# Strassen products for 44 of the 72 blocks of an input projection, with one pool of tiles that all phases share

## The chip, the cores and the metric

The kernel runs on one core of one Trainium2 chip. The metric is the device time of one execution in microseconds (us). The core has TensorE (PE: matrix multiplies; PEld are its weight loads), VectorE (DVE), ScalarE (ACT), GpSimd (POOL) and SyncE (SP, which here issues the loads). They run beside each other, each through its own instructions in order, and wait for each other on semaphores.

## The reference

One decoder block on 512 tokens with 16 meta tokens ahead of them (528 columns), 1024 channels. Cut to what matters:

```python
u = rmsnorm(h, attn_norm_w)
proj = u @ w_in                                   # 1024 -> 9 x 1024
q, f_raw, i_in, g_out, b_gate, c_gate, x_conv, gate_a, gate_b = split(proj)
q = silu(q);  f = lb + (1 - lb) * sigmoid(f_raw);  k = 1 - f;  v = i_in
o = rmsnorm(hgrn2_chunked(q, k, v, log(f)), hgrn_norm_w)   # 8 heads, gated linear recurrence
y_a = o * silu(g_out)
y_b = b_gate * causal_dwconv(c_gate * x_conv, conv_w)      # width 3
h = h + (sigmoid(gate_a) * y_a + sigmoid(gate_b) * y_b) @ w_out
a, val = split(rmsnorm(h, ffn_norm_w) @ w_up)              # 1024 -> 2 x 2816
h = h + (silu(causal_dwconv(a, ffn_conv_w, ffn_conv_b)) * val) @ w_down
return rmsnorm(h, final_norm_w)[meta tokens dropped]
```

## The kernel before

Channels lie on the 128 partitions, tokens along the columns. All is float32. For a matrix multiply each operand is split into a high part, rounded to TensorE's fp32r, and a low part, the rest: `h = copy(x)` on ACT, `lo = x - h` on DVE. A product then takes three matmuls (high by high, high by low, low by high).

A **unit** is 128 output channels of one of the nine parts of w_in: 1024 x 128 weights, fetched with one DMA into `wr`, split into `wh` and `wl`. `w_in` has 72 units. `mtile` (L133) multiplies a unit with the 8 tiles `uh`, `ul` of the input (128 channels each, scaled by the norm's weight but not yet by its reciprocal root `rstd`) in two column spans of 256 to 264: 8 x 3 x 2 = 48 matmuls. The result, in one of the two 1024-wide accumulators `psm` of the pool `pmain`, is multiplied by `rstd` on DVE as it is taken out (`evac`, L155).

The program has these stages.

- Start: loads, the first three units (f, q, i of head 0), and `rstd`.
- Scan: for head j from 0 to 7, `fqi(j + 1)` runs the units f, q, i of the next head and `mix(j)` the units b, c, x, g, ga, gb of this one. The recurrence `recur(j)`, a generator with eight pieces of small matmuls, DVE products and masked copies, is woven in: `tick` takes its next piece after every few matmul groups.
- Output projection (L589): 8 units of w_out on the merged heads `mh`, `ml`, then the second norm.
- Feed-forward: 6 pairs of units of w_up by `mtile`, then 16 pairs as **Strassen pairs** (`pair_weights` L666, `product` L733, `Pair` L747): two units, each split in two along the 1024 inputs, are computed over two halves of the tokens with seven half-size products of 12 matmuls instead of eight. That needs sums of weight blocks (S1 to S4) and combinations of the input halves (`ch`, `cl`, from `combos`, L627), each split into high and low. The products go to three accumulators r1, r2, r3; r1 is added to again after a copy of it was kept (c1, c2, c3 by `keep`, L742). Between products, `more` puts blocks of the down projection.

A scheduler, not the text of the program, sets the final order on each engine: it places ready instructions by priority, so loads and splits of weights, and pieces of the recurrence, move ahead of where they are written.

Of the kernel before, what the change touches and what calls it, by code (L numbers as in the profile page):

```python
# [7 lines left out]
F32 = mybir.dt.float32  # L8
# [28 lines left out]
def unit_order():  # L37
    out = [(n, 0) for n in ("f", "q", "i")]
    for j in range(KT):
        if j + 1 < KT:  # L40
            out += [(n, j + 1) for n in ("f", "q", "i")]
        out += [(n, j) for n in ("b", "c", "x", "g", "ga", "gb")]
    return out
# [12 lines left out]
def block_kernel(ctx: ExitStack, tc: tile.TileContext, xT, par, wts, pairs, ident, masks, finw, out):  # L56
# [68 lines left out]
    mains = [pmain]  # L125
# [77 lines left out]
    xt = [xpool.tile([P, L], F32, name=f"xt{k}", tag=f"xt{k}") for k in range(KT)]  # L203
# [62 lines left out]
    mg_pool = ctx.enter_context(tc.tile_pool(name="mg", bufs=1, side="right"))  # L266
    mh = [mg_pool.tile([P, 516], F32R, name=f"mh{k}", tag=f"mh{k}")[:, :LT] for k in range(KT)]
    ml = [mg_pool.tile([P, 516], F32R, name=f"ml{k}", tag=f"ml{k}")[:, :LT] for k in range(KT)]
    ph = ExitStack()
    p1 = ph.enter_context(tc.tile_pool(name="ph1", bufs=1))  # L270
    z0 = [p1.tile([P, L], F32, name=f"z0{i}") for i in range(2)]
    uh = [p1.tile([P, L], F32R, name=f"uh{k}", tag=f"uh{k}") for k in range(KT)]
    ul = [p1.tile([P, L], F32R, name=f"ul{k}", tag=f"ul{k}") for k in range(KT)]
    rstd = p1.tile([P, L], F32, name="rstd")
    Ks = [p1.tile([P, L + 1], F32, name=f"K{i}") for i in range(2)]
    Vs = [p1.tile([P, L + 1], F32, name=f"V{i}") for i in range(2)]
    Fs = [p1.tile([P, L + 1], F32, name=f"F{i}") for i in range(2)]
    As = [p1.tile([P, NCH, P], F32, name=f"A{i}") for i in range(2)]
    Qs = [p1.tile([P, LT], F32, name=f"Q{i}") for i in range(2)]
    cx = p1.tile([P, LC], F32, name="cx")  # L280
    for i in range(2):
        nc.gpsimd.memset(Ks[i][:, L:], 0.0)
        nc.gpsimd.memset(Vs[i][:, L:], 0.0)
        nc.gpsimd.memset(Fs[i][:, L:], 1.0)
        nc.gpsimd.memset(As[i], 0.0)

    with tc.tile_pool(name="rp0", bufs=1) as rp:
        acc = rp.tile([P, L], F32, name="acc")
        firsts = [(split_unit(raw, 4), new_ps()) for raw, _ in heads]
        sides = ((FULL, L, z0[0]), (PART, LT, z0[1][:, :LT]))  # L290
        for k in range(KT):
            if k % 2 == 0:
                firsts[0][0][2][k // 2]()
            split_scaled(uh[k], ul[k], xt[k], pr("attn", k))
            if k % 2 == 0:
                firsts[1][0][2][k // 2]()
            for ((h, lo, _), ps), (spans, _, _) in zip(firsts, sides):
                mm3(ps, h[:, k, :], lo[:, k, :], uh[k], ul[k], spans, k == 0, k == KT - 1)
# [5 lines left out]
        for (_, ps), (spans, _, z) in zip(firsts, sides):  # L304
            act.copy(z, res(ps, spans))
        banks = [pqk.tile([P, NCH * P], F32, name="psq", tag="psq") for _ in range(2)]
        spread_rstd(rstd, acc, lambda i: banks[i], rp, L)
        act.copy(Vs[0][:, :L], res(mtile(uh, ul, FULL, (h3rd, l3rd)), FULL))
    p2 = ph.enter_context(tc.tile_pool(name="ph2", bufs=2))

    def sig(src, n):
        s = p2.tile([P, n], F32, name="sg", tag="sg")
        act.activation(s, src, AF.Sigmoid)
        return s

    def fqi(j):
        b = j % 2
        if j:
            ps = mtile(uh, ul, FULL)
            z = p2.tile([P, L], F32, name="z", tag="z")  # L320
            evac(ps, FULL, z, rstd)
        else:
            z = z0[0]
            dve.tensor_tensor(z, z, rstd, op=ALU.mult)
        s = sig(z, L)
        dve.tensor_scalar(Fs[b][:, :L], s, lbc[:, j:j + 1], lb[:, j:j + 1], op0=ALU.mult, op1=ALU.add)
        act.activation(Ks[b][:, :L], Fs[b][:, :L], AF.Identity, bias=one1, scale=-1.0)
        if j:
            ps = mtile(uh, ul, PART)
            z = p2.tile([P, L], F32, name="z", tag="z")[:, :LT]  # L330
            evac(ps, PART, z, rstd[:, T0:])
        else:
            z = z0[1][:, :LT]
            dve.tensor_tensor(z, z, rstd[:, T0:], op=ALU.mult)
        s = sig(z, LT)
        dve.tensor_tensor(Qs[b], z, s, op=ALU.mult)
        if j:
            ps = mtile(uh, ul, FULL)
            evac(ps, FULL, Vs[b][:, :L], rstd)
        else:  # L340
            dve.tensor_tensor(Vs[b][:, :L], Vs[b][:, :L], rstd, op=ALU.mult)
# [3 lines left out]
    def recur(j, oS):  # L345
        b = j % 2
        K, V, F, Q, A = Ks[b], Vs[b], Fs[b], Qs[b], As[b]
# [137 lines left out]
    def mix(j, oS):  # L485
        r = rstd[:, T0:]
        ps = mtile(uh, ul, PART)
        yb = p2.tile([P, LT], F32, name="yb", tag="yb")
        evac(ps, PART, yb, r)
        rc = rstd[:, TC:]  # L490
        ps = mtile(uh, ul, CONV)
        evac(ps, CONV, cx, rc)
        ps = mtile(uh, ul, CONV)
        z = p2.tile([P, L], F32, name="z", tag="z")[:, :LC]
        evac(ps, CONV, z, rc)
        dve.tensor_tensor(cx, cx, z, op=ALU.mult)
        acc = p2.tile([P, LT], F32, name="cacc", tag="cacc", bufs=1)
        dve.tensor_scalar(acc, cx[:, 2:], pr("conv", 3 * j + 2), None, op0=ALU.mult)
        for d in (1, 2):
            dve.scalar_tensor_tensor(acc, cx[:, 2 - d:LC - d], pr("conv", 3 * j + 2 - d), acc,  # L500
                                     op0=ALU.mult, op1=ALU.add)
        dve.tensor_tensor(yb, yb, acc, op=ALU.mult)
        ps = mtile(uh, ul, PART)
        z = p2.tile([P, L], F32, name="z", tag="z")[:, :LT]
        evac(ps, PART, z, r)
        s = sig(z, LT)
        ga = p2.tile([P, LT], F32, name="gacc", tag="gacc")
        dve.tensor_tensor(ga, z, s, op=ALU.mult)
        ps = mtile(uh, ul, PART)
        z = p2.tile([P, L], F32, name="z", tag="z")[:, :LT]  # L510
        evac(ps, PART, z, r)
        s = sig(z, LT)
        dve.tensor_tensor(ga, ga, s, op=ALU.mult)
        ps = mtile(uh, ul, PART)
        while pending:
            if next(pending[0], "end") == "end":
                pending.pop(0)
        z = p2.tile([P, L], F32, name="z", tag="z")[:, :LT]
        evac(ps, PART, z, r)
        s = sig(z, LT)  # L520
        dve.tensor_tensor(yb, yb, s, op=ALU.mult)
        dve.tensor_tensor(ga, ga, oS, op=ALU.mult)
        dve.tensor_tensor(ga, ga, yb, op=ALU.add)
        split(mh[j], ml[j], ga)

    fqi(0)
    for j in range(KT):
        oS = p2.tile([P, LT], F32, name="oS", tag="oS")
        beat[:] = ([-10, 6] if j == 0 else [0, 7] if j + 1 < KT else [0, 5])
        pending.append(recur(j, oS))  # L530
        if j + 1 < KT:
            fqi(j + 1)
        mix(j, oS)

    ph.close()
    scan.close()
    pairs_ps = ExitStack()
# [6 lines left out]

    ch, cl = {}, {}
    homes = [(mg_pool, f"m{s}{k}") for s in "hl" for k in range(KT)]
    homes += [(fp1, f"cb{i}") for i in range(12)]
    fa, val, gs = {}, {}, {}
    gp0 = ctx.enter_context(tc.tile_pool(name="gp0", bufs=1))
    slots = []  # L550

    def more_slots(pool, n):
        for _ in range(n):
            i = len(slots)
            slots.append((pool.tile([P, SEQ], F32R, name=f"gh{i}"), pool.tile([P, SEQ], F32R, name=f"gl{i}")))

    more_slots(gp0, G0)

    up = ExitStack()
    vpool = up.enter_context(tc.tile_pool(name="vpool", bufs=1))  # L560
    vh = [vpool.tile([P, LT], F32R, name=f"vh{k}", tag=f"vh{k}") for k in range(KT)]
    vl = [vpool.tile([P, LT], F32R, name=f"vl{k}", tag=f"vl{k}") for k in range(KT)]
# [36 lines left out]


    for c in (4, 0, 5, 1, 3, 6, 2):
        for t in (ch, cl):
            for jp in range(2):
                pool, tag = homes.pop()
                t[c, jp] = pool.tile([P, 2, HW], F32R, name=f"cmb{len(homes)}", tag=tag)
    hp = ctx.enter_context(tc.tile_pool(name="hp", bufs=1, side="right"))
    hn = {}
    A, B = slice(0, HW), slice(LT - HW, LT)

    def norm(h, j):  # L610
        k = 4 * h + j
        if j % 2 == 0:
            if h == 0:
                hn["t"] = hp.tile([P, 4 * LT], F32, name="hn", tag="wt", bufs=2)
            hn[h, j // 2] = hn["t"][:, h * 2 * LT:(h + 1) * 2 * LT].rearrange("p (j n) -> p j n", j=2)
        dve.scalar_tensor_tensor(hn[h, j // 2][:, j % 2, :], xt[k][:, T0:], pr("ffn", k), rstd2,
# [309 lines left out]
```

## Time and profile before

| | |
|---|---|
| runs shown | 926.48, 926.55 and 1101.75 us, median 926.55 |
| profiled execution | 925.9 us |
| its span, first to last instruction | 924.1 us, which leaves 1.8 us around it |
| granted TensorE clock, mean | 0.997 |
| PE / DVE / ACT busy | 912.9 / 649.3 / 405.5 us |
| DMA | 91.24 MB, 99 GB/s on average |

Busy time is the union of an engine's instructions. In a timeline row the first number is the start in us from the start of the span, the second the length. The stages lie at about 0 to 29.7 us (start), 29.7 to 509 (scan), 509 to 555 (output projection), 555 to 630 (first feed-forward pairs), 630 to 881 (Strassen pairs and down projection), and the tail.

### The profile page before, as it was taken

The page shows a single profiled execution, that of the slowest core. Times are in us where ns is not written, and L with a number is a line of the kernel's source. Part 1 is how long each engine was busy: PE and PEld are TensorE (multiplying, and loading weights), DVE is VectorE, ACT ScalarE, POOL GpSimd, SP SyncE. Part 2 cuts the span into 40 slices and gives each one's busy share as a digit, 9 for nine tenths or more (in the row PEclk, how much of TensorE's full clock was granted, in tenths as well). Part 3 has the DMA queues.
Part 4 walks back from the last instruction along what each step waited for, and adds up shares of the span by engine and source line. Part 5 has one row for each costly group of instructions (what it writes and reads, how often), then busy time and mean ns, then how long its engine had stood idle before and what let it go on. Part 6 is the DMA issues. An engine that isn't in the chain of part 4 may idle for free.

```text
span 924.1 us, 16735 instructions
## 1 busy us (share of the span) xinstructions
PE 912.9 (99%) x6864; PEld 870.3 (94%) x6864; DVE 649.3 (70%) x1268; ACT 405.5 (44%) x677; POOL 25.4 (3%) x101
## 2 busy tenths in 40 slices
PE   9999999999999999999999999999999999999996
PEld 8999999999999999999999999999999999999984
DVE  7876856857658559467575556995777878787655
ACT  8524325234243253342424435545545454545433
POOL 0400100001000001000000000000000000000000
PEclk9999999999999999999999999999999999999998
DMA  7322222322322222222222221443525353433312
GB/s 264 123 69 70 88 73 69 90 73 69 91 70 70 91 70 69 91 70 70 72 89 69 91 93 47 137 141 98 173 94 180 93 167 107 147 127 114 93 45 92
DMA packets 29597, 91.24 MB, mean 99 GB/s; under 512 B 3280, under 2 KB 4560, under 8 KB 29520
## 3 DMA queue, kind: packets, MB, share of 16 engines
q1 hardware_dynamic: 29232, 89.64, 30.4%
q8 instruction: 54, 0.88, 0.4%
q10 hardware_dynamic: 288, 0.52, 0.3%
q14 instruction: 23, 0.19, 0.1%
HBM read 88.06 MB, written 2.10 MB: 98 GB/s over the span
## 4 chain that ended last, share of the span: by engine, by line
PE 97%; ACT 1%; DVE 1%; DMA 0%; SPq 0%; issue 0%; ACTq 0%; DVEq 0%
PE psm L106 20%; PE psm L109 19%; PE psm L107 19%; PE pr L738 6%; PE pr L740 6%; PE pr L739 6%; PE psm L794 4%; PE psm L795 4%; PE psm L796 4%; PE psq L399 3%; PE po L468 1%; PE po L467 1%; PE psq L451 1%; PE psq L424 1%; PE psq L479 0%; DMA wr<-in_wts 0%
## 5 line engine op out<-in xcount | busy, mean ns | idle before, releaser
L106 PE MATMUL psm<-uh,wh 128*128 128x258 f32 (+2 forms) x1152 | 309.8, 290 | 0.6 <-ACT uh L151 0.6
L107 PE MATMUL psm<-ul,wh 128*128 128x258 f32 (+2 forms) x1152 | 302.7, 283 | 0.4 <-DVE ul L152 0.2
L109 PE MATMUL psm<-uh,wl 128*128 128x258 f32 (+2 forms) x1152 | 233.0, 283 | 0.0
L106 PEld LDWEIGHTS psm<-uh,wh 128*128 128x128 f32 x1152 | 218.5, 190 | 3.3 <-issue 1.8
L107 PEld LDWEIGHTS psm<-ul,wh 128*128 128x128 f32 x1152 | 217.1, 188 | 0.8 <-DVE ul L152 0.8
L86 ACT CAST wh<-wr 128x1024 fp32r<-128x1024 f32 (+1 forms) x120 | 120.7, 1008 | 201.4 <-PE psm L107 152.5
L109 PEld LDWEIGHTS psm<-uh,wl 128*128 128x128 f32 x1152 | 177.6, 188 | 0.0
L87 DVE TENSOR_TENSOR wl<-wr,wh 128x1024 fp32r<-128x1024 f32 (+1 forms) x120 | 140.0, 1169 | 34.3 <-ACT wh L86 28.7
L738 PE MATMUL pr<-cmb,wh 128*128 128x258 f32 x448 | 127.2, 284 | 0.3 <-ACT xt L726 0.3
L740 PE MATMUL pr<-cmb,wl 128*128 128x258 f32 x448 | 126.6, 283 | 0.0
L739 PE MATMUL pr<-cmb,wh 128*128 128x258 f32 x448 | 126.5, 282 | 0.0
L155 DVE TENSOR_TENSOR z<-psm,rstd 128x514 f32<-128x514 f32 (+2 forms) x46 | 32.2, 699 | 78.4 <-PE psm L109 78.4
L738 PEld LDWEIGHTS pr<-cmb,wh 128*128 128x128 f32 x448 | 84.7, 189 | 2.2 <-ACT xt L726 0.7
L739 PEld LDWEIGHTS pr<-cmb,wh 128*128 128x128 f32 x448 | 85.0, 190 | 1.4
L740 PEld LDWEIGHTS pr<-cmb,wl 128*128 128x128 f32 x448 | 84.4, 189 | 0.0
L794 PE MATMUL psm<-wh,gh 128*128 128x512 f32 x176 | 69.4, 397 | 1.1 <-DVE vf L853 1.1
L795 PE MATMUL psm<-wl,gh 128*128 128x512 f32 x176 | 69.5, 395 | 0.0
L796 PE MATMUL psm<-wh,gl 128*128 128x512 f32 x176 | 69.3, 395 | 0.0
L681 ACT CAST wh<-wt 128x1024 fp32r<-128x1024 f32 x32 | 33.6, 1049 | 51.1 <-PE psm L796 31.0
L682 DVE TENSOR_TENSOR wl<-wt,wh 128x1024 fp32r<-128x1024 f32 x32 | 39.1, 1221 | 22.4 <-ACT wh L681 22.4
L416 DVE COPY_PREDICATED A<-mk_t,psq 128x192 f32<-128x192 int32 x144 | 47.4, 357 | 6.7 <-PE psq L399 5.8
L106 PE MATMUL psm<-vh,wh 128*128 128x256 f32 (+2 forms) x144 | 44.2, 322 | 0.0
(224 smaller groups left out, 1380.6 us busy)
## 6 DMA issues: line engine op xcount, KB each, us to landing
wr<-in_wts SPq DMA_DIRECT2D x112, 512.0 KB, 3.5
wt<-in_pairs SPq DMA_DIRECT2D x16, 512.0 KB, 4.0
wt<-in_pairs SPq DMA_DIRECT2D x32, 256.0 KB, 4.8
wr<-in_pairs SPq DMA_DIRECT2D x16, 512.0 KB, 4.2
xt<-in_xT SPq DMA_DIRECT2D x8, 264.0 KB, 4.5
out<-xt SPq DMA_DIRECT2D x8, 256.0 KB, 2.2
wr<-in_wts SPq DMA_DIRECT2D x8, 128.0 KB, 3.9
fw<-in_finw ACTq DMA_DIRECT2D x2, 256.0 KB, 3.8
```

Source lines behind the costliest of these rows:

```text
L86: act.copy(h[:, i:i + n, :], raw[:, i:i + n, :])
L87: dve.tensor_tensor(lo[:, i:i + n, :], raw[:, i:i + n, :], h[:, i:i + n, :].bitcast(F32), op=ALU.subtract)
L106: pe.matmul(o, wh, rh[:, a:b], start=first, stop=False)
L107: pe.matmul(o, wh, rl[:, a:b], start=False, stop=False)
L109: pe.matmul(o, wl, rh[:, a:b], start=False, stop=last)
L416: dve.copy_predicated(a4[:, :, :, (4 - r) * m:], mk.unsqueeze(1).to_broadcast([P, 2, nb, r * m]), ps[:, :, lo_:hi_].rearrange("p c (b x) - ...
L738: pe.matmul(ps, h[:, j], ch[c, j // 2][:, j % 2], start=a, stop=False, skip_group_check=True)
L739: pe.matmul(ps, h[:, j], cl[c, j // 2][:, j % 2], start=False, stop=False, skip_group_check=True)
L740: pe.matmul(ps, lo[:, j], ch[c, j // 2][:, j % 2], start=False, stop=z, skip_group_check=True)
L794: pe.matmul(o, gh, wh, start=first, stop=False)
L795: pe.matmul(o, gh, wl, start=False, stop=False)
L796: pe.matmul(o, gl, wh, start=False, stop=last)
```

## The change

**Strassen pairs in the scan.** Head 0's units f, q, i, c, x, b, gb are computed as before, on the input without `rstd` (`raw_unit`). From then on the input is normalised fully (`normed`) and 22 pairs of units run as Strassen pairs over token halves of 264: (f, q) of heads 1 to 7, (c, x) of heads 1 to 7, (g, ga) of heads 0 to 7. The other 21 units (i, b, gb) run as single units on the halves (`half_unit`). `Pair` gets a sink (`FQ`, `CX`, `GA`, and `Up` for the feed-forward) that takes the results out, and its `fill` is empty in the scan. The signs of the Strassen scheme change so that combinations of weights and inputs need no negated copies.

```diff
-def unit_order(): ...
+FIRST = [("f", 0), ("q", 0), ("i", 0), ("c", 0), ("x", 0), ("b", 0), ("gb", 0)]
+SINGLE = [("i", 1)] + [u for j in range(1, KT) for u in ([("i", j + 1)] if j + 1 < KT else []) + [("b", j), ("gb", j)]]
+PAIRS = [("f", "q", 1), ("g", "ga", 0)]
+for _j in range(1, KT):
+    PAIRS += ([("f", "q", _j + 1)] if _j + 1 < KT else []) + [("c", "x", _j), ("g", "ga", _j)]
...
+        def middle(self):
+            w, r1, r2, r3, n = self.w, self.r1, self.r2, self.r3, self.width
+            c1 = keep(r1, "c1", n)
+            product(r2, w["M12"], "U21", True)
+            self.sink.n1a(r2, c1)
+            product(r1, w["S2"], "D6", False)
+            self.c2 = keep(r1, "c2", n)
+            product(r3, w["S1"], "D5", True)
+            self.fill()
+            product(r1, w["S3"], "D7", False)
+            self.sink.n2b(r3, keep(r1, "c3", n))
+            self.fill()
+        def last(self):
+            product(self.r1, self.w["M22"], "D4", False)
+            self.sink.n2a(self.r1)
+            product(self.r3, self.w["S4"], "U22", False)
+            self.sink.n1b(self.r3, self.c2)
...
+    def prepare():
+        hns = []
+        for jp in range(2):
+            hns.append(normed(lambda k: xt[k], "attn", rstd, L, jp))
+            yield
+        works = [combos(hns[jp], jp, HL, L, True) for jp in range(2)]
...
-    fqi(0)
-    for j in range(KT):
-        ...
+    items = [("s", value(1)), ("p", lambda: FQ(1)), ("p", lambda: GA(0)), ("m", 0)]
+    for j in range(1, KT):
+        if j + 1 < KT:
+            items += [("p", lambda j=j: FQ(j + 1)), ("s", value(j + 1))]
+        items += [("p", lambda j=j: CX(j)), ("p", lambda j=j: GA(j)), ("s", b_gate(j)),
+                  ("s", lambda j=j: b_merge(j)), ("m", j)]
...
+        elif kind == "p":
+            w = pair_weights()
+            nxt = Pair(w, arg(), HL, lambda: None)
+            if cur:
+                cur.last()
+            cur = nxt
+            cur.middle()
```

**Shared tiles.** A pool `big` of 40 tiles of 528 columns (`home`) holds, one after the other, the input `xt`, the raw `uh` and `ul`, the combinations (`cm`), the merged heads, their splits, and the feed-forward's tiles. So the input is loaded a second time after the last pair, the merged heads are split only once the combinations' tiles come free, and there is one tile `V_t` and one `oS` instead of two. The normalised halves `hn` take both tiles of the tag `wt`, which also receives a pair's weights. In the scan the four PSUM banks of `psm` become r1 (twice), r2 and r3; a single unit uses r2's bank for its first half and one of r1's for its second.

```diff
+    def home(i, dtype=F32, n=528, name="t"):
+        return big.tile([P, 528], dtype, name=f"{name}{i}", tag=f"b{i}")[:, :n]
+    def pbank(i):
+        return ppair.tile([P, 512], F32, name="pr", tag=f"pr{i}", bufs=1 + (i == 0))
...
+    xt = [home(k, name="xr") for k in range(KT)]
+    for k in range(KT):
+        load_x(k)
+    for k in range(KT):
+        mh.append(home(24 + k, F32R, LT, "mh"))
+        ml.append(home(32 + k, F32R, LT, "ml"))
+        split(mh[k], ml[k], merged[k])
```

How the order changes on the engines is seen at two places. The first is DVE behind the moment at which `rstd` is known. Before, these rows follow (line numbers of the kernel before; `z00`, `z01` are f and q of head 0):

```order
L324 TENSOR_TENSOR z00_210<-z00_210,rstd_228 128x528
L334 TENSOR_TENSOR z01_211<-z01_211,rstd_228 128x514
L341 TENSOR_TENSOR V0_231<-V0_231,rstd_228 128x528
L326 TENSOR_SCALAR F0_233<-sg_503,lbc_178,lb_177 128x528
L336 TENSOR_TENSOR Q0_237<-z01_211,sg_508 128x514
L155 TENSOR_TENSOR z_568<-psm_519,rstd_228 128x528
L391 TENSOR_TENSOR qv_699<-Q0_237,F0_233 128x4x32 x2
```

DVE goes from f, q and i straight into the recurrence of head 0 (`qv`). In the changed kernel (its own line numbers) the same point reads so, where `hn` are the normalised halves:

```order
L772 TENSOR_TENSOR F0_214<-F0_214,rstd_210 128x528
L772 TENSOR_TENSOR Q0_218<-Q0_218,rstd_210 128x528
L772 TENSOR_TENSOR V_213<-V_213,rstd_210 128x528
L400 SCALAR_TENSOR_TENSOR hn_526<-xt0_80,par_t_79,rstd_210 128x528
L400 SCALAR_TENSOR_TENSOR hn_526<-xt4_84,par_t_79,rstd_210 128x528
```

The normalisation now stands between f, q, i and the recurrence. Further on, between pieces of that recurrence (`K0`, `T128`), the last combinations (`ct`, `cm`) stand ahead of the first pair's weights (`wt` sums at L303 and L304, low halves `wl` at L293):

```order
L389 TENSOR_TENSOR ct_974<-hn_583 128x528
L303 TENSOR_TENSOR wt_1006<-wt_1006 128x512
L561 TENSOR_TENSOR K0_211<-K0_211,T22_932 128x4x64
L363 TENSOR_TENSOR cm23_961<-ct_974,cm22_960 128x528
L304 TENSOR_TENSOR wt_1006<-wt_1006,wr_1004 128x512
L563 TENSOR_TENSOR T128_1057<-T22_932 128x4
L634 TENSOR_TENSOR F1_215<-pr_1033,c1_1062 128x264
L308 TENSOR_TENSOR s4_1021<-wt_1006,wr_1004 128x512
L293 TENSOR_TENSOR wl_1018<-wt_1006,wh_1017 128x1024
```

The combinations and the pair's sums have come in between head 0's last pieces on DVE: from the first of the rows at L772 to `wl_1018` DVE has 117 instructions, 32 of norm and combinations, 57 of the recurrence, 21 of taking results out and 7 of weights.

The second place is PE at the recurrence's transposes of K (`psq`, L441 before). Before, they stand within a unit (`psm_933`), between matmuls that read the same weights `wh_928` and `wl_929` and the next tiles of the input:

```order
L106 MATMUL psm_933<-uh5_217,wh_928 128x258
L107 MATMUL psm_933<-ul5_225,wh_928 128x258
L109 MATMUL psm_933<-uh5_217,wl_929 128x258 x2
L441 MATMUL psq_970<-id_t_88,K0_229 128x128 x3
L442 MATMUL psq_970<-id_t_88,K0m_696 17x128
L106 MATMUL psm_933<-uh6_218,wh_928 128x258
L107 MATMUL psm_933<-ul6_226,wh_928 128x258
L106 MATMUL psm_933<-uh6_218,wh_928 128x258
```

Now they stand in the first pair, (f, q) of head 1, behind the products of its blocks M11 and M12 and ahead of those of its sums S2 and S1: `pr_1033`, `pr_1032` and `pr_1034` are its r2, r1 and r3, `wl_1011` and `wl_1018` the low halves of the blocks and of the sums.

```order
L320 MATMUL pr_1033<-cm34_503,wl_1011 128x264
L570 MATMUL psq_1103<-id_t_88,K0_211 128x128 x3
L571 MATMUL psq_1103<-id_t_88,K0m_743 17x128
L318 MATMUL pr_1032<-cm2_790,wh_1017 128x264
L319 MATMUL pr_1032<-cm3_791,wh_1017 128x264
L318 MATMUL pr_1034<-cm0_788,wh_1017 128x264
L319 MATMUL pr_1034<-cm1_789,wh_1017 128x264
L320 MATMUL pr_1032<-cm2_790,wl_1018 128x264
```

What follows the transposes on PE is no longer the rest of a unit whose weights the matmuls ahead of it have read already, but the first product that reads the sums' halves `wh_1017` and `wl_1018`.

More of the change, by code (lines that the diff above doesn't have):

```diff
@@ new lines, in product, with keep @@
+    def product(ps, w, c, start):
+        h, lo = w
+        for j in range(4):
+            ch, cl = cmb[c, j // 2]
+            ch, cl = ch[:, j % 2], cl[:, j % 2]
+            pe.matmul(ps, h[:, j], ch, start=start and j == 0, stop=False, skip_group_check=True)
+            pe.matmul(ps, h[:, j], cl, start=False, stop=False, skip_group_check=True)
+            pe.matmul(ps, lo[:, j], ch, start=False, stop=j == 3, skip_group_check=True)
+            if j % 2:
+                tick()
+    def keep(r, n, w):
+        c = hp.tile([P, HL], F32, name=n, tag="c1" if n == "c3" else n)[:, :w]
+        act.copy(c, r)
+        return c
@@ L285, in block_kernel, with raw3, raw_unit @@
         nc.gpsimd.memset(As[i], 0.0)
+    HALF = (slice(0, HL), slice(HL, L))
+    def raw3(o, wh, wl, rh, rl, first, last):
+        pe.matmul(o, wh, rh, start=first, stop=False)
+        pe.matmul(o, wh, rl, start=False, stop=False)
+        pe.matmul(o, wl, rh, start=False, stop=last)
+    def raw_unit(unit, sink):
+        h, lo = unit
+        for i, at in enumerate(HALF):
+            o = pbank(1 - i)[:, :HL]
+            for k in range(KT):
+                raw3(o, h[:, k, :], lo[:, k, :], uh[k][:, at], ul[k][:, at], k == 0, k == KT - 1)
+                if k % 2:
+                    tick()
+            sink(o, at)
@@ L287, in block_kernel, with half_unit @@
+    def half_unit(unit, i, sink):
+        h, lo = unit
+        o = pbank(1 - i)[:, :HL]
+        for k in range(KT):
+            rh, rl = cmb[(("U11", "U12"), ("U21", "U22"))[k // 4][i], k % 4 // 2]
+            raw3(o, h[:, k, :], lo[:, k, :], rh[:, k % 2], rl[:, k % 2], k == 0, k == KT - 1)
+            if k % 2:
+                tick()
+        sink(o, HALF[i])
     with tc.tile_pool(name="rp0", bufs=1) as rp:
         acc = rp.tile([P, L], F32, name="acc")
-        firsts = [(split_unit(raw, 4), new_ps()) for raw, _ in heads]
@@ L517, in mix @@
                 pending.pop(0)
[L518 to L524, printed above, removed]
-    fqi(0)
[L527 to L530, printed above, removed]
-        if j + 1 < KT:
-            fqi(j + 1)
-        mix(j, oS)
+        g = ga[j]
@@ new lines, in merge, with times, sink @@
+        merged[j] = home(8 + j, n=LT, name="mg")
+        dve.tensor_tensor(g[:, T0:], g[:, T0:], oS[j], op=ALU.mult)
+        dve.tensor_tensor(merged[j], g[:, T0:], y[j], op=ALU.add)
+    def times(dst):
+        def sink(o, at):
+            dve.tensor_tensor(dst[:, at], o, rstd[:, at], op=ALU.mult)
+        return sink
+    names = ["U11", "U21", "U22", "U12"]
+    for q, c in enumerate(["U12", "U11", "U21", "U22"]):
+        for jp in range(2):
+            cmb[c, jp] = [home(24 + 4 * q + 2 * jp + h, F32R, name="cm").rearrange("p (j n) -> p j n", j=2)
+                          for h in range(2)]
@@ new lines, in block_kernel, with some, x_sink @@
+    work = [prepare()]
+    def some(n):
+        for _ in range(n):
+            next(work[0], None)
+    for dst in (Fs[0], Qs[0], V_t):
+        dve.tensor_tensor(dst[:, :L], dst[:, :L], rstd, op=ALU.mult)
+    decay(0)
+    s = ring()
+    act.activation(s, Qs[0], AF.Sigmoid)
+    dve.tensor_tensor(Qs[0], Qs[0], s, op=ALU.mult)
+    cx0, x0 = ring("cx", 1), ring()
+    def x_sink(o, at):
+        times(x0)(o, at)
+        dve.tensor_tensor(cx0[:, at], cx0[:, at], x0[:, at], op=ALU.mult)
+        if at is hi_:
+            y[0] = conv(0, cx0)
@@ new lines, in b0_sink, with gb0_sink @@
+    def b0_sink(o, at):
+        z = ring()
+        times(z)(o, at)
+        i, t = parts(at)
+        dve.tensor_tensor(y[0][:, t], y[0][:, t], z[:, at][:, i], op=ALU.mult)
+    def gb0_sink(o, at):
+        z = ring()
+        times(z)(o, at)
+        act.activation(z[:, at], z[:, at], AF.Sigmoid)
+        i, t = parts(at)
+        dve.tensor_tensor(y[0][:, t], y[0][:, t], z[:, at][:, i], op=ALU.mult)
+    for q, sink in enumerate((times(cx0), x_sink, b0_sink, gb0_sink)):
+        unit = ahead.pop()
+        ahead.append(load_unit())
+        some(1)
+        raw_unit(unit, sink)
+        some(1)
+        if q == 0:
+            beat[:] = [-4, 6]
+            begin(0)
@@ L598, in block_kernel @@
         first()
[L601 to L616, printed above, removed]
-                                 op0=ALU.mult, op1=ALU.mult)
@@ new lines, in block_kernel, with prepare2 @@
+    tags = [home(i, F32R, 2 * HW, "cf") for i in range(24, 40)]
+    tags = [fp1.tile([P, 528], F32R, name=f"cb{i}")[:, :2 * HW] for i in range(12)] + tags
+    for c in ("U11", "U21", "U22", "D5", "D6", "D4", "D7"):
+        for jp in range(2):
+            cmb[c, jp] = [tags.pop(0).rearrange("p (j n) -> p j n", j=2) for _ in range(2)]
+    def prepare2():
+        for jp in range(2):
+            hn = normed(lambda k: xt[k][:, T0:], "ffn", rstd2, LT, jp)
+            yield
+            yield from combos(hn, jp, HW, LT, False)
@@ L901 @@
     early = wup[:EARLY].reshape(2 * EARLY, P, KT, P)
[L902 to L905 removed]
+    pairs += [halves(*wup[i]) for i in range(EARLY, NF)]
     pairs = np.ascontiguousarray(np.stack(pairs))
```

471 lines of the change are left out of this document (250 added, 221 removed).

## The prediction

> **What bounds the kernel now.** Three views, in this order: the page's busy times and its chain of waits, then busy times by stretch, then single rows of the timeline for durations.
>
> ```profile
> PE 912.9 (99%) x6864; PEld 870.3 (94%) x6864; DVE 649.3 (70%) x1268; ACT 405.5 (44%) x677; POOL 25.4 (3%) x101
> PE 97%; ACT 1%; DVE 1%; DMA 0%; SPq 0%; issue 0%; ACTq 0%; DVEq 0%
> ```
>
> PE works through 99% of the span and makes 97% of the chain that ended last. So a matmul less is worth its time wherever PE does not come to wait, and the question is where it will. The busy times by stretch (start and end in us; busy time of PE, PEld, DVE, ACT and POOL with instruction counts in brackets; clock; DMA share; GB/s) say which engine has room in the scan:
>
> ```profile
> 30.00:40.00 10.00, 10.00 (x85) 9.99 (x84) 9.60 (x25) 7.26 (x11) 4.59 (x9) 1.00 0.18 52
> 40.00:50.00 10.00, 10.00 (x81) 10.00 (x80) 9.76 (x36) 2.70 (x5) 4.90 (x12) 1.00 0.27 95
> 50.00:60.00 10.00, 10.00 (x81) 10.00 (x80) 9.39 (x33) 2.10 (x3) 0.00 (x0) 1.00 0.34 107
> 60.00:70.00 10.00, 10.00 (x90) 9.76 (x89) 4.38 (x7) 3.04 (x6) 0.00 (x0) 1.00 0.17 52
> 100.66:412.63 311.97, 311.97 (x2542) 306.54 (x2541) 207.87 (x491) 115.21 (x210) 11.58 (x51) 1.00 0.24 77
> 915.00:924.00 9.00, 1.31 (x6) 0.74 (x4) 3.55 (x13) 2.37 (x5) 0.00 (x0) 0.72 0.31 117
> ```
>
> Two readings. Over five heads (100.66 to 412.63, 62.4 us each) DVE works 41.6 us a head and ACT 23.0, so both have room. But from 30 to 60 us, behind `rstd`, DVE is at 94 to 98% already: head 0's recurrence and the results of the first units arrive at once, and PE is not held only because it has ready units to go on with. Whatever is added to DVE there moves everything behind it.
>
> **What PE saves.** A matmul's price is the spacing of starts, since they are pipelined:
>
> ```profile
> 29.67 0.28 PE L106 MATMUL psm<-uh,wh 128*128 128x264 f32 x1
> 33.09 0.29 PE L106 MATMUL psm<-uh,wh 128*128 128x256 f32 x1
> 38.85 0.38 PE L350 MATMUL psq<-id_t,V 128*128 128x128 f32 x2
> ```
>
> Between the first two rows lie 28 matmuls 264 wide: 3.42 / 28 = 0.122 us each. The 48 matmuls of the unit of 256 and 258 columns up to the third row give 5.76 / 48 = 0.120. Before, 72 units x 48: two of nine parts (f, i) have two spans of 264, the other seven 256 and 258, so 8 x (96 x 0.122 + 336 x 0.120) = 416.3 us. Now, 28 single units x 48 and 22 pairs x 7 products x 12 make 3192 matmuls, all 264 wide: 389.4 us. **-26.9 us**, the cheaper count less the wider spans. A steady head goes from 62.4 us, of which 52.0 are units and 10.4 the recurrence, to (3 x 48 + 3 x 84) x 0.122 + 10.4 = 58.7.
>
> **What DVE gets in a steady head.** DVE's instructions overlap their neighbours too:
>
> ```profile
> 29.73 0.71 DVE L324 TENSOR_TENSOR z<-z,rstd 128x528 f32<-128x528 f32 x1 [0.69 <-ACT rstd L200]
> 30.36 0.69 DVE L334 TENSOR_TENSOR z<-z,rstd 128x514 f32<-128x514 f32 x1
> L87 DVE TENSOR_TENSOR wl<-wr,wh 128x1024 fp32r<-128x1024 f32 x112 | 136.9, 1222 | 34.1 <-ACT wh L86 28.7 <-issue 0.3
> L682 DVE TENSOR_TENSOR wl<-s,wh 128x512 fp32r<-128x512 f32 x16 | 11.0, 686 | 0.0
> L692 DVE TENSOR_TENSOR wt<-wt 128x512 f32<-128x512 f32 x32 | 21.7, 686 | 4.2 <-DMA wt<-in_pairs 4.2
> L760 DVE TENSOR_TENSOR fa<-pr,c 128x258 f32<-128x258 f32 x16 | 6.7, 419 | 0.7 <-PE pr L740 0.7
> ```
>
> The first starts 0.63 us ahead of the second though it lasts 0.71: I take 0.085 off every duration where rows stand back to back. A low half of 1024 then costs 1.14, one of 512 or a sum of blocks 0.60, taking out half a unit 0.34. A pair needs three halves of 1024, one of 512 and four sums (6.4 us) where two units needed two halves (2.3): +4.1, three times a head, +12.3. Against that V, the decay and the split of the merged head leave DVE (V and decay for ACT, the split for the end), about -3.8 by the instructions of a head. So 41.7 + 8.5 = 50.2 of 58.7 us, 86%, and ACT about 30. DVE does not become the bound on average. But it has less to give back when a masked copy, the states S or `on`, on which PE's next recurrence step waits, stand behind a low half of 1.2 us. I find 0 to 1 us a head, take half a microsecond: **+3.5** over seven heads (bounds 0 and 8).
>
> **The start, where DVE was full.** The normalisation and the combinations are new here, and the first pair's weights come here too. Their prices are bounded by the same operations in the feed-forward, two tiles of 264 being as wide as two of 258 to 2%:
>
> ```profile
> L616 DVE SCALAR_TENSOR_TENSOR hn<-xt,par_t,rstd 128x514 f32<-128x514 f32 x8 | 5.5, 749 | 0.0
> L622 DVE TENSOR_TENSOR cmb<-ct,cmb 128x516 fp32r<-128x516 f32 x8 | 5.4, 691 | 0.0
> L633 DVE TENSOR_TENSOR ct<-hn 128x516 f32<-128x516 f32 x4 | 2.8, 692 | 0.0
> 29.53 0.17 ACT L200 COPY rstd<-psq 128x16 f32<-128x16 f32 x1
> 61.84 0.42 DVE L432 TENSOR_TENSOR K<-K,T 128x256 f32<-128x256 f32 x1
> ```
>
> Before, DVE came to the last product of head 0's K (L432) 32.1 us after its first instruction behind `rstd`. The changed order has, up to `wl_1018` just behind that K: 8 norms (5.4), 8 differences (5.2) and 16 low halves (9.9), together +20.5; two low halves and four sums of the pair, +4.7; three low halves of units fewer, -3.4; head 1's first two levels, 21 instructions, not there yet, -5.1; and taking out results in halves, +2.1. So 32.1 + 18.8 = 50.9 us, and the sums' product may start at 29.7 + 50.9 = **80.6**.
>
> PE's own work ahead of that product: the first four units end at 33.1 as before, x, b, gb and i of head 1 take 4 x 48 x 0.122 = 23.4, the products of M11 and M12 2.9, and head 0's recurrence up to the transposes of K 5.7, from these rows (three levels of 1.30 each, and for the transposes the price of those of V at L350 again):
>
> ```profile
> 39.02 0.44 PE psq L350 x4
> 39.45 0.11 PE pm L354
> 43.98 1.30 PE psq L399 x8
> 60.85 0.61 PE psq L424 x8
> 61.46 0.18 PE pm L427 x4
> ```
>
> That is 65.1. PE waits 80.6 - 65.1 = 15.5 us up to this product, in pieces, at the masked copies of the three levels above all, for DVE is late there already. Behind it DVE has 27.6 us of work to the end of head 0 and PE about 23, so it stays late a little: 1 to 3, taken as 2. Weights may add to this: the first pair's two loads go to tiles that `hn` holds until its last difference (`ct_974`), and these loads take
>
> ```profile
> wt<-in_pairs SPq DMA_DIRECT2D x16, 512.0 KB, 4.0
> wt<-in_pairs SPq DMA_DIRECT2D x32, 256.0 KB, 4.8
> ```
>
> 4 to 5 us, against some 5 us in which DVE does other work: 0 to 2, taken at nothing. **+17.5** for the start. It is bounded below at 7, if half of the 20.5 us of norm and combinations turns out to be hidden, as where DVE's idle 5.6 us between 60 and 70 would be used first, and above at 27, if the full durations instead of the spacings hold (117 x 0.085 = 10 us more).
>
> [...] In the quietest rows of the tail the clock is 0.72 where the scan has 1.00. [...]
>
> **Other edits, near nothing.** Taking copies c1 to c3 on ACT between products:
>
> ```profile
> L744 ACT COPY c<-pr 128x258 f32<-128x258 f32 x48 | 17.7, 369 | 16.3 <-PE pr L740 16.1
> L86 ACT CAST wh<-wr 128x1024 fp32r<-128x1024 f32 x112 | 117.7, 1051 | 201.0 <-PE psm L107 152.5 <-issue 21.0 <-PE pr L739 15.8
> L173 ACT ACT_TABLE_LOAD x11 | 14.1, 1283 | 0.2
> ```
>
> A copy (0.37) has one product (12 x 0.122 = 1.46 us) to hide in, since `fill` is empty in the scan. Behind one cast it takes 1.42 and still fits; behind a table load 1.65, and PE waits 0.2. Behind two casts it would be 1.0 late; this is the third rival. The second load of the input stands in SP's queue behind the last unit's weights and is asked for some 18 us later: nothing. The split of the eight merged heads moves to the end of the scan, where the last pair's U12, U21 and U22 must first come free: the last heads' splits, 0.6 each on DVE, may lie ahead of the first output unit; **+1** (0 to 4). In the feed-forward only signs change: 0, give or take 2.
>
> **Sum**, against the profiled execution's 925.9 us (924.1 span and 1.8 around it; the median shown is 926.55, so 0.65 above): 925.9 - 26.9 + 17.5 + 3.5 + 1 = **921.0 us**.
>
> **Rivals.**
> - *The gain stays.* The start's wait is 2 us at most: PE's queue has enough pieces that need no DVE, or DVE takes the added work faster. For it: DVE idles 5.6 us between 60 and 70, PE's first eight units need none of the new work. Against it: 30 to 60 us, where DVE has 1.3 us free and 18.8 come in. 925.9 - 26.9 + 2 + 3.5 + 1 = 905.5, **905**.
> - *Slower: no filler between products.* In every pair of the scan the c1 to c3 copies stand behind two casts, or the sums of blocks behind DVE's recurrence, and PE waits 1.3 us a pair. For it: pairs of the feed-forward had blocks of the down projection between products, these have none, and ACT's casts (1.05) are on the same queue as the copies. Against it: ACT has work for only half of a head. 22 x 1.3 = 28.6 in place of the 3.5: 921 - 3.5 + 28.6 = **946**. From 1.25 us a pair upwards (27.6 / 22) the time is beyond 2%.
> - *The change does less than it says*: a count of matmuls that stays. The order of the changed kernel has 3192 of them in the input projection, so I give this no chance; the row price of 0.122 already holds for 264 columns.
>
> **How the numbers follow.** The forecast 0.72, gain stays 0.15, slower 0.13. The forecast's own range is 925.9 - 26.9 + 7 = 906 to 925.9 - 26.9 + 27 + 8 + 4 + 2 = 940. For 8 in 10 the range reaches down to the first rival and up to the edge of the second: 904 to 945. 2% of the median, 18.5 us, is about what a measurement of this kernel tells from no change: below 908 is faster, above 945 slower. Nearly all of the first rival and the lowest part of the forecast are below 908: 0.14. Most of the second rival lies above 945: 0.12. The rest, 0.74, is within.
>
> **What would show it.** PE's count 264 lower and its busy time about 27 lower (the matmuls' price). In the stretch 30 to 85 us, DVE at over 95% and PE idle by 12 to 18 us, released by DVE; head periods near 59 us behind it, with DVE at 86% (the two DVE sums). Starts of the first pair's S2 product near 81. No wait on ACT's `c` tiles of over 0.5 us in a pair. The prediction is wrong if PE's idle time lies evenly over all pairs (the second rival), or if 30 to 85 us show PE full (the first).

## The result, and the profile after

The changed kernel takes 915.45 us (median of four runs, 915.32 to 916.16) against 926.52; the ratio is 0.9882 with an interval of 0.9863 to 0.9902. One run of the kernel before took 1101.75 us and does not enter the ratio. The change is 1.2% faster: within 2%, as forecast, and 5.5 us below the 921.0 of the prediction. The profiled execution took 916.16 us (914.3 span), so against the 925.9 of before the prediction's sum has to explain 9.7 us.

The page's busy times and the shares of the chain of waits, after:

```profile
PE 891.3 (97%) x6600; PEld 845.0 (92%) x6600; DVE 729.2 (80%) x1452; ACT 488.0 (53%) x859; POOL 34.0 (4%) x100
PE 88%; DVE 7%; ACT 3%; DMA 1%; issue 1%; SPq 0%; ACTq 0%; DVEq 0%
```

PE's count is 264 lower, and DVE and ACT have come into the chain. Busy time by stretch says where (start and end; busy time of PE, PEld, DVE, ACT, POOL; clock; DMA share; GB/s):

```profile
60.00:70.00 10.00, 5.93 (x49) 5.00 (x47) 9.45 (x34) 4.16 (x11) 0.00 (x0) 0.97 0.08 13
70.00:80.00 10.00, 5.31 (x25) 4.65 (x26) 8.71 (x17) 3.82 (x7) 0.00 (x0) 0.67 0.55 172
231.09:289.82 58.73, 58.58 (x473) 57.35 (x473) 49.37 (x117) 32.72 (x64) 3.60 (x10) 1.00 0.36 109
```

From 60 to 80 us PE is busy for 11.2 of 20 us while DVE is at 91%, and PE's clock is 0.67 in the second half of it. A steady head (last row) has PE full and DVE at 49.4 of 58.7. Over the stretch that the prediction names, and for the two spells in which the clock was down:

```profile
30.00:85.00 55.00, 45.55 (x329) 42.93 (x328) 52.41 (x123) 25.27 (x48) 5.05 (x10) 0.91 0.26 83
69.70:72.95 3.25, 3.01 (x14) 3.01 (x15) 3.00 (x6) 0.41 (x2) 0.00 (x0) 0.51 0.93 283
76.65:83.10 6.45, 4.45 (x17) 3.69 (x18) 5.95 (x10) 4.04 (x7) 0.00 (x0) 0.50 0.76 246
```

PE's waits from 25 to 85 us, by who ended them; from 113 to 500 us it waits for nothing:

```profile
PE psq L570 <- DVE K L561: 3.2, 1, 3.2
PE pr L320 <- DVE wl L293: 2.6, 1, 2.6
PE pr L318 <- ACT wh L292: 1.5, 1, 1.5
PE psq L553 <- DVE A L545: 1.5, 1, 1.5
PE pr L423 <- DVE wl L94: 0.4, 1, 0.4
PE psq L528 <- DVE qv L522: 0.3, 1, 0.3
```

All but the 0.4 (the low half of a single unit) are waits for the recurrence's steps or for the first pair's halves. The chain of waits shows the heads' periods by the first level of each recurrence, and the first matmul of the output projection closes the scan:

```profile
113.72 1.30 PE psq L528 x8
...
407.25 1.30 PE psq L528 x8
```

```profile
L113 PE MATMUL psm<-mh,wh x128: 276/280/287, 499.5 to 545.3; 128*128 128x256 f32 x64, 128*128 128x258 f32 x64
```

Heads take 58.7 us, (407.25 - 113.72) / 5, to the tenth what the matmuls' count gave. The output projection's main matmuls run from 499.5 to 545.3, where they ran from 509.1 to 554.4 before:

```profile
L106 PE MATMUL psm<-mh,wh x128: 277/282/286, 509.1 to 554.4; 128*128 128x256 f32 x64, 128*128 128x258 f32 x64
```

So the scan and its start gave 9.6 us. With a saving of 26.9 that is a loss of **17.3 us**, and since the heads from 113.7 on lose nothing, all of it lies ahead of there. The projection then takes 0.5 us longer, and the rest 0.7 less.

The first pair's product that reads the sums' halves is the row at 79.73 of the second block. Ahead of it stands DVE's first row behind `rstd`, behind it what ACT and DVE do from 72.5 to 74 us:

```profile
30.88 0.71 DVE L772 TENSOR_TENSOR F<-F,rstd 128x528 f32<-128x528 f32 x1 [0.75 <-ACT rstd L207]
```

```profile
69.94 0.59 PE L320 MATMUL pr<-cm,wl 128*128 128x264 f32 x1 [2.58 <-DVE wl L293]
70.33 0.42 PE L318 MATMUL pr<-cm,wh 128*128 128x264 f32 x1
70.55 0.42 PE L319 MATMUL pr<-cm,wh 128*128 128x264 f32 x1
...
73.66 0.28 PE L320 MATMUL pr<-cm,wl 128*128 128x264 f32 x1
77.12 0.88 PE L570 MATMUL psq<-id_t,K 128*128 128x128 f32 x3 [3.18 <-DVE K L561]
...
79.73 0.59 PE L318 MATMUL pr<-cm,wh 128*128 128x264 f32 x1 [1.51 <-ACT wh L292]
80.11 0.42 PE L319 MATMUL pr<-cm,wh 128*128 128x264 f32 x1
80.33 0.42 PE L318 MATMUL pr<-cm,wh 128*128 128x264 f32 x1
...
80.99 0.59 PE L320 MATMUL pr<-cm,wl 128*128 128x264 f32 x1
...
83.50 0.28 PE L319 MATMUL pr<-cm,wh 128*128 128x264 f32 x1
```

```profile
72.54 0.38 ACT L326 COPY c<-pr 128x264 f32<-128x264 f32 x1 [3.13 <-PE pr L320]
72.82 1.17 ACT L361 CAST cm<-ct 128x528 fp32r<-128x528 f32 x2
73.49 0.71 DVE L363 TENSOR_TENSOR cm<-ct,cm 128x528 fp32r<-128x528 f32 x1 [0.79 <-ACT cm L361]
```

79.7 - 65.1 = 14.6 us late. Behind the gaps of 2.58 and 3.18 us the matmuls start every 0.22 us (70.33 to 70.55, 80.11 to 80.33), at 83.50 every 0.12 again. The first of the two slow spells, from 69.7 to 73 us, is followed by a wait of 3.2 us for K, so PE's own delay in it is covered. But DVE idles 0.79 us behind it: ACT's next cast of a combination (L361) stands behind the copy of the product that ran slowly (L326). So this spell cost 0.8 us at most.

### The profile page after: what moved, and what is told of

The parts are those of the page before. It is cut to its first block, busy times and chain, and to the rows that moved or that the text cites. A ratio compares the mean times of both kernels' runs of the same rounds, so it can differ in the third digit from the quotient of the medians.

```text
span 914.3 us, 16721 instructions
## 1 busy us (share of the span) xinstructions
PE 891.3 (97%) x6600; PEld 845.0 (92%) x6600; DVE 729.2 (80%) x1452; ACT 488.0 (53%) x859; POOL 34.0 (4%) x100
## 4 chain that ended last, share of the span: by engine, by line
PE 88%; DVE 7%; ACT 3%; DMA 1%; issue 1%; SPq 0%; ACTq 0%; DVEq 0%
PE pr L318 14%; PE pr L319 13%; PE pr L320 13%; PE psm L983 4%; PE pr L421 4%; PE psm L985 4%; PE psm L984 4%; PE pr L422 4%; PE pr L423 4%; PE psm L116 4%; PE psm L114 4%; PE psm L113 4%; PE psq L528 3%; DMA wr<-in_wts 1%; ACT L180 1%; ACT junk L599 1%
## 5 line engine op out<-in xcount | busy, mean ns | idle before, releaser
L318 PE MATMUL pr<-cm,wh 128*128 128x264 f32 x616 | 180.9, 294 | 1.7 <-ACT wh L292 1.5
L320 PE MATMUL pr<-cm,wl 128*128 128x264 f32 x616 | 175.4, 286 | 2.6 <-DVE wl L293 2.6
L319 PE MATMUL pr<-cm,wh 128*128 128x264 f32 x616 | 176.5, 287 | 0.0
L94 DVE TENSOR_TENSOR wl<-wr,wh 128x1024 fp32r<-128x1024 f32 (+1 forms) x76 | 86.2, 1138 | 45.7 <-ACT wh L93 43.0
L318 PEld LDWEIGHTS pr<-cm,wh 128*128 128x128 f32 x616 | 117.2, 190 | 4.3 <-ACT wh L292 2.0
L320 PEld LDWEIGHTS pr<-cm,wl 128*128 128x128 f32 x616 | 117.1, 191 | 3.1 <-DVE wl L293 3.0
L293 DVE TENSOR_TENSOR wl<-wt,wh 128x1024 fp32r<-128x1024 f32 x76 | 92.8, 1223 | 30.5 <-ACT wh L292 30.3
L319 PEld LDWEIGHTS pr<-cm,wh 128*128 128x128 f32 x616 | 117.1, 190 | 0.0
L421 PE MATMUL pr<-cm,wh 128*128 128x264 f32 x336 | 98.3, 293 | 0.0
L422 PE MATMUL pr<-cm,wh 128*128 128x264 f32 x336 | 96.0, 286 | 0.0
L423 PE MATMUL pr<-cm,wl 128*128 128x264 f32 x336 | 95.1, 283 | 0.4 <-DVE wl L94 0.4
L326 ACT COPY c<-pr 128x264 f32<-128x264 f32 (+1 forms) x114 | 42.6, 374 | 58.8 <-PE pr L320 57.2
L318 PE MATMUL pr<-cf,wh 128*128 128x258 f32 x256 | 72.5, 283 | 0.0
L319 PE MATMUL pr<-cf,wh 128*128 128x258 f32 x256 | 72.1, 282 | 0.0
L320 PE MATMUL pr<-cf,wl 128*128 128x258 f32 x256 | 71.9, 281 | 0.0
L423 PEld LDWEIGHTS pr<-cm,wl 128*128 128x128 f32 x336 | 63.2, 188 | 0.6 <-DVE wl L94 0.6
L421 PEld LDWEIGHTS pr<-cm,wh 128*128 128x128 f32 x336 | 63.3, 188 | 0.3 <-DVE z L739 0.2
L422 PEld LDWEIGHTS pr<-cm,wh 128*128 128x128 f32 x336 | 63.2, 188 | 0.0
L293 DVE TENSOR_TENSOR wl<-wr,wh 128x1024 fp32r<-128x1024 f32 x38 | 46.5, 1223 | 10.7 <-ACT wh L292 10.7
L318 PE MATMUL pr<-cb,wh 128*128 128x258 f32 x192 | 54.7, 285 | 0.3 <-ACT xr L944 0.3
```

What stands on the lines that cost most here:

```text
L94: dve.tensor_tensor(lo[:, i:i + n, :], raw[:, i:i + n, :], h[:, i:i + n, :].bitcast(F32), op=ALU.subtract)
L293: dve.tensor_tensor(lo, src, h.bitcast(F32), op=ALU.subtract)
L318: pe.matmul(ps, h[:, j], ch, start=start and j == 0, stop=False, skip_group_check=True)
L319: pe.matmul(ps, h[:, j], cl, start=False, stop=False, skip_group_check=True)
L320: pe.matmul(ps, lo[:, j], ch, start=False, stop=j == 3, skip_group_check=True)
L326: act.copy(c, r)
```

## The experiments

Theory: DVE's queue behind `rstd` (recurrence of head 0, normalisation, combinations, first pair) makes the whole loss. Rivals: the first pair's form or its weights (loads into the tiles of `hn`, ACT's casts), a price of its own in every pair, and DVE's small slack in every head.

**Taking the low halves of the combinations out of DVE.** The subtraction goes, and the products read the high half in its place:

```diff
+            if ps.shape[-1] == HL:
+                cl = ch
...
+    def total_low(n):
+        return n != HL
...
     def plain(c, src, jp, n):
...
+        act.copy(cmb[c, jp][0], src)
+        if total_low(n):
+            dve.tensor_tensor(cmb[c, jp][1], src, cmb[c, jp][0].bitcast(F32), op=ALU.subtract)
```

> Left out: the 16 low halves of the combinations on DVE (the products read the high half twice instead, so PE's matmuls stay the same in number). Theory: the loss at the start is DVE's queue behind rstd. 16 x 0.62 = 9.9 us leave it, PE's wait up to the product of the first pair's sums falls from 14.6 by as much, and the gap in which the clock fell (2 us) may go too: 903.5 to 906 us. Rival: the first pair waits for its weights, which are loaded to tiles that the normalised halves hold, or for ACT's casts; then only the last two reads move, 912.5 to 915.5 us.

902.26 us, ratio 0.9742 (0.9727 to 0.9756): 13.2 us less than the change, more than the 9.9 of the subtractions and 1.2 below the range that was expected. Busy time by stretch, then PE's waits from 30 to 120 us:

```profile
60.00:70.00 10.00, 9.33 (x77) 8.24 (x76) 10.00 (x24) 6.79 (x14) 0.00 (x0) 1.00 0.44 131
70.00:80.00 10.00, 10.00 (x82) 9.74 (x82) 9.79 (x17) 6.43 (x14) 0.00 (x0) 1.00 0.76 244
```

```profile
PE pr L322 <- DVE wl L293: 0.7, 1, 0.7
PE psq L613 <- DVE on L608: 0.6, 1, 0.6
PE psq L533 <- DVE qv L527: 0.2, 1, 0.2
PE pr L320 <- ACT c L328: 0.2, 1, 0.2
```

The clock stays at 1.00, so what the slow spells had cost went too. DVE comes to the sums' low halves at 67.1 instead of 79.7, 12.6 earlier for 9.9 of work: the rest is in the 1.8 us that it had been idle from 60 to 80 us, waiting for PE and for ACT's high halves, and something under 1 us that stays open. The rival of the weights falls: the sums moved with DVE's queue, and in the changed kernel none of DVE's idle time from 60 to 84 us ends with a load.

**More for PE to do meanwhile.** The pair (f, q) of head 1 as two single units, with the combinations between the units rather than ahead of them; in the second kernel (g, ga) of head 0 too:

```diff
-    items = [("s", value(1)), ("p", lambda: FQ(1)), ("p", lambda: GA(0)), ("m", 0)]
+    items = [("s", lambda: f_one(1)), ("s", lambda: q_one(1)), ("s", value(1)), ("p", lambda: GA(0)), ("m", 0)]
...
             unit = ahead.pop() if ahead else load_unit()
+            if q < 2:
+                ahead.append(load_unit())
...
-            some(99)
+            some(1)
             half_unit(unit, 1, sink)
+            some(1 if q < 2 else 99)
```

> The pair (f, q) of head 1 runs as two single units on the normalised halves, and the combinations stand between the units. Theory: PE gets 11.7 us of units to do while DVE works through the combinations; DVE gets 3.6 us more ahead of the first pair's sums, so the wait falls by about 8; 12 matmuls more cost 1.5 us: 906 to 909 us, with 5 to 7 us of waits left. Rival: what costs is the first pair itself, in whatever place (its sums, its loads, no filler between its products); then the wait moves to (g, ga) of head 0 undiminished: 916 to 918 us.

> The pairs (f, q) of head 1 and (g, ga) of head 0 both run as single units. Theory: PE has 23 us more ahead of the first pair, which then stands behind all of the combinations' work; nearly no wait and no clock drop are left, 24 matmuls more cost 2.9 us: 902 to 906 us. Rival as for the other: 917 to 919 us.

905.3 us (ratio 0.9771, 0.9754 to 0.9787), just below the 906 to 909 that were expected, and 905.19 (0.9771, 0.9756 to 0.9785). What PE still waits for from 30 to 162 us in the first of them, 1.9 us where 5 to 7 were expected:

```profile
PE psq L608 <- DVE on L603: 0.6, 1, 0.6
PE psq L528 <- DVE qv L522: 0.5, 2, 0.3
PE pr L320 <- DVE wl L293: 0.4, 1, 0.4
PE pr L423 <- DVE wl L94: 0.4, 1, 0.4
```

The wait did not move with the first pair: it is not the pair's form. Both are 10 us faster than the changed kernel with 12 and 24 matmuls more. Which part of the 10 us comes from the units and which from the combinations' new place between them was not separated. The second pair turned into units buys nothing further: PE's waits over the same stretch are 1.7 us, and where its 12 matmuls, 1.46 us, are made up for is not shown. These are the fastest versions that leave nothing out, 2.3% below the kernel before and 1.1% below the change.

**What the clock cost.** 26 matmuls whose result nobody reads stand in the gap ahead of the transposes of K:

```diff
             self.sink.n1a(r2, c1)
+            if next_pair[0] == 1:
+                idle = pmisc.tile([P, 512], F32, name="pm", tag="pm")[:, :HL]
+                for _ in range(26):
+                    pe.matmul(idle, w["M12"][0][:, 3], cmb["D4", 1][0][:, 1], start=True, stop=True)
             product(r1, w["S2"], "D6", False)
```

> 26 matmuls of no use (12 x 264 wide ones' worth of 0.122 us each, 3.2 us) stand in PE's gap ahead of the transposes of K, at 74 to 77 us, and nothing else is changed. [...]

The theory was that the second slow spell comes of this gap, so that with the gap filled the time falls to 913 to 914 us; if the matmuls behind it are slow for another reason, or DVE hides the time, 915.2 to 916. It is 913.7 us, 1.75 below the change. The runs differ: three took 913.62 to 913.78 us at a mean clock of 0.996, one, the profiled one, 915.51 at 0.994 (the changed kernel: 0.990 to 0.992). In that one the gap is filled and the clock falls all the same, a little later (and once ahead of the filler, at 69.9, as in the changed kernel):

```profile
72.65 3.60 PE L345 MATMUL pm<-cm,wh 128*128 128x264 f32 x26
76.23 0.52 PE L574 MATMUL psq<-id_t,K 128*128 128x128 f32 x3
...
78.44 0.39 PE L318 MATMUL pr<-cm,wh 128*128 128x264 f32 x1 [1.27 <-ACT wh L292]
78.66 0.28 PE L319 MATMUL pr<-cm,wh 128*128 128x264 f32 x1
...
79.70 0.39 PE L320 MATMUL pr<-cm,wl 128*128 128x264 f32 x1 [0.51 <-DVE wl L293]
...
80.24 0.42 PE L320 MATMUL pr<-cm,wl 128*128 128x264 f32 x1
80.46 0.42 PE L318 MATMUL pr<-cm,wh 128*128 128x264 f32 x1
```

At 78.66 the next matmul follows 0.12 us later, at 80.24 0.22 us later; the gaps ahead of it are 1.3 us (up to 78.44) and 0.5 us (up to 79.70). The other three runs have no trace; that they lack this second spell is argued from their clock (0.002 of 912 us is 1.8 us) and their time. So the second spell cost 1.8 to 1.9 us. In the profiled run it stands behind gaps of 1.3 and 0.5 us, as the first spell of the changed kernel stands behind the 2.6 us ahead of 69.94. How long a gap has to be to bring a spell on, and why one run of four had the second, these runs do not show.

**DVE's slack in a steady head.** Four subtractions of 512 columns more in every pair from the third on, into a scratch tile:

```diff
             dve.tensor_tensor(lo, src, h.bitcast(F32), op=ALU.subtract)
+            if names[0] in ("M12", "M22") and 3 <= next_pair[0] <= 22:
+                for a in (0, 4):
+                    dve.tensor_tensor(extra, src[:, a:a + 4], h[:, a:a + 4].bitcast(F32), op=ALU.subtract)
```

> From the third pair of the scan on each pair has four more subtractions of 512 columns on DVE that write a scratch tile nobody reads: 4 x 0.60 = 2.4 us a pair, 7.2 us a steady head, so DVE goes from about 50.2 to 57.4 of the head's 58.7 us; from the sums at the same spacing. Theory: what is asked of DVE in a steady head is asked early enough, so the average alone counts: 915.5 to 917 us. Rival (the step of the prediction that took 0.5 us a head): PE's recurrence steps wait wherever DVE has little to give back, and with 1.3 us left they do so by 1 us a head or more: 921 us and above.

918.75 us (ratio 0.9919, 0.9903 to 0.9936), 3.3 above the change and between the two ranges that were expected. Its busy time in one head, and PE's waits from 113 to 480 us:

```profile
348.00:407.00 59.00, 58.71 (x475) 57.48 (x475) 55.31 (x131) 32.88 (x64) 4.45 (x10) 1.00 0.34 108
```

```profile
PE psq L612 <- DVE on L607: 2.3, 6, 0.6
PE psq L532 <- DVE qv L526: 0.8, 1, 0.8
```

With DVE at 94% of a head PE begins to wait at one place, for `on`, 0.4 us a head; without the addition, at 84%, nowhere. The theory that the average alone counts was too smooth, and the rival's 1 us a head too high.

**The price of a pair.** The pairs (g, ga) of heads 2 to 6 as single units:

```diff
+        if 2 <= j <= 6:
+            items += [("s", lambda j=j: g_one(j)), ("s", lambda j=j: ga_one(j))]
+        else:
+            items += [("p", lambda j=j: GA(j))]
```

> The pairs (g, ga) of heads 2 to 6 run as two single units each. Theory: the pair's worth is its 12 matmuls less at 0.122 us and nothing else (no wait in it), so five times 1.46: 915.5 + 7.3 = 922.8 us, give or take 1. Rival: pairs cost waits of their own (copies between products with no filler), of 0.7 us or more each: 919.5 us or less.

922.6 us, 7.15 above the change: 1.43 a pair, against 12 x 0.122 = 1.46. The chain shows it:

```profile
172.55 1.30 PE psq L528 x8
...
232.74 1.30 PE psq L528 x8
```

60.2 us a head instead of 58.7. A steady pair has no wait of its own: the slower rival of the prediction falls.

**The combinations' low halves on POOL**, which is busy for 5 us from 30 to 85, in the changed kernel and in the one with (f, q) of head 1 as units:

```diff
-                dve.tensor_tensor(t, src, cmb[c, jp][0].bitcast(F32), op=ALU.subtract)
+                (nc.gpsimd if n == HL else dve).tensor_tensor(t, src, cmb[c, jp][0].bitcast(F32), op=ALU.subtract)
```

> The 16 low halves of the combinations are computed by POOL instead of DVE; nothing is left out. Theory: DVE's queue is the cause, so 9.9 us less in it gives what leaving them out gave, if POOL does one of them in under 1.5 us: 902 to 906 us. Rival: POOL takes longer or slows DVE beside it, and PE waits for POOL instead, at the first products that read the low halves and at the recurrence's steps that POOL has behind them: 909 us and above.

> The pair (f, q) of head 1 as single units and the low halves of the combinations on POOL, both together. Theory: what the units left of waits (905.3 us, about 1.5 us of waits and some spacing) goes too: 903 to 905 us. Rival: POOL is the slower one and holds the single units: 907 us and above.

919.24 us (ratio 0.9927, 0.9911 to 0.9943) and 919.15 (0.9925, 0.991 to 0.994): both miss, slower than without POOL by 3.8 and by 13.9 us. The rival holds, and rows of the first show how DVE is slowed. One of POOL's groups, then one run of POOL's subtractions and DVE beside it, and last the same DVE product in the changed kernel:

```profile
L363 POOL TENSOR_TENSOR cm<-ct,cm 128x528 fp32r<-128x528 f32 x8 | 12.7, 1603 | 14.1 <-ACT cm L361 14.1
```

```profile
39.09 7.28 POOL L363 TENSOR_TENSOR cm<-hn,cm 128x528 fp32r<-128x528 f32 x5 [2.67 <-ACT cm L361]
```

```profile
40.69 1.56 DVE L781 TENSOR_TENSOR cx<-cx,z 128x264 f32<-128x264 f32 x1
42.18 0.42 DVE L739 TENSOR_TENSOR z<-pr,rstd 128x264 f32<-128x264 f32 x1
```

```profile
L781 DVE TENSOR_TENSOR cx<-cx,z x2: 415/418/420, 41.4 to 41.8; 128x264 f32<-128x264 f32 x2
```

POOL needs 1.6 us for what DVE does in 0.62. And while it runs, the DVE product `cx` with both inputs in SBUF lasts 1.56 us, about as long as one of POOL's (7.28 / 5 = 1.46), where it takes 0.42 without POOL, and where the one of the same size with an input from PSUM (`z`) still takes 0.42. So DVE lost more than it was spared: from 30 to 85 us the groups of its instructions that both traces have there in the same number take 59.7 us instead of 45.7 (number times mean), 13.9 more, and the 16 subtractions that it was spared had taken 11.4.

## Why the prediction was right, and what in it was off

Against the profiled 916.16 the sum was 4.9 too high, and by term:

- **-26.9 for PE: right.** 58.7 us a head was forecast and measured, and five pairs turned back cost 1.43 us each where 1.46 was worked out. PE's busy time fell by 21.6 only, not by about 27, since matmuls that are held up or run at the lower clock count as busy for longer: 0.138 us each from 30 to 85 us (45.55 / 329), where before the change it was 0.121 from 30 to 60 us (30.00 / 247). The heads' period was the better witness.
- **+17.5 for the start: 17.3, and in the right place.** The sums' product was to start at 80.6 and starts at 79.7, 14.6 us late instead of 15.5. Two kernels that give DVE less or PE more to do there get 13.2 and 10.1 us back. That the start comes out to 1 us is in part luck. DVE's queue began at 30.88, not 29.7, and the sums' low halves are first read at 80.99: 50.1 us, 1.8 of them idle, where 50.9 of work had been added up. The product itself begins ahead of them, at 79.73, as soon as ACT's cast of the high halves lets it. PE's idle time from 30 to 85 us is 9.5 us (8.0 ended by DVE, 1.5 by ACT), where 12 to 18 had been forecast; the rest of the lateness lies in matmuls that count as busy, held up or at half clock. And one piece was wrong: the 2 us behind that product were put down to DVE staying late, and most of what was lost there is the clock (1.8 to 1.9), with 0.6 for `on`. The sum has no term for the clock. One belonged in, in place of the other.
- **+3.5 for the steady heads: 0.** This is the step that failed most: half a microsecond a head for DVE's low halves ahead of the recurrence's steps. PE waits nowhere from 113 to 500 us. DVE's 49.4 us of busy time in a head had been forecast as 50.2, so the load was right and the price of it not: it takes 94%, not 84%, before 0.4 us a head appear.
- **+1 for the end of the scan and 0 for the feed-forward: 0.5 and -0.7.** One wait of 0.4 for the low half of a merged head, and a feed-forward shorter by 0.7, whose cause is open.

3.5 + 1.2 + 0.2 are the 4.9 us. Of the rivals, the gain that stays needed the start's wait gone, and the experiments reach it only with work left out or moved: 905 was its number, and 905.2 to 905.3 is what the rearranged kernels take, by the means that it named, more work for PE that does not hang on DVE's added work. That the numbers meet is luck: the rival has 3.5 us for the steady heads, which cost nothing, and none for the 12 or 24 matmuls more. The copies c1 to c3 between products, the slower rival, cost nothing in the steady heads, though `fill` is empty; in the first pair one of them held up ACT's cast and with it DVE, by 0.8 us at most.

## What to carry to other kernels

An engine that idles 20 or 30% on average can still be the bound in one stage, as DVE was here: busy for 70% of the run before and 80% after, and for 52.4 of the 55 us from 30 to 85. Ahead of a change that adds work to it, read its busy share by stretch, sum its queue up to the first instruction that the bound engine will wait for, and compare with the bound engine's own work up to the same point: here this gave 15.5 us where 14.6 were measured, with errors of about 1 us either way in it. Then look for work of the bound engine that needs none of the new results and put it there: giving up 1.5 us of the saving for two units at the right place, with the added work spread between them, brought 10 us.

## What the runs showed of the hardware

- POOL did not come for free beside DVE: while POOL ran its subtractions of 528 columns (1.46 us each), a DVE product of 264 columns with two SBUF inputs took 1.56 us, 0.42 without them, and one of the same size with a PSUM input took 0.42 beside them.
- The clock was down to half (0.51 and 0.50) behind gaps of 2.6 and of 3.2 us in the changed kernel, and in one run with the filler matmuls behind 1.3 and 0.5 us; matmuls of 264 columns then started every 0.22 us instead of 0.12. The two spells of the changed kernel lasted 3.25 and 6.45 us. The filler's runs put the price of the second at 1.8 to 1.9 us; the first, behind which PE came to wait 3.2 us for DVE, 0.8 at most.
